# Attention stage A/B of a streaming encoder: the planner's TensorE order replaced by one written out by hand, with row-half scores

## The chip, the cores and the metric

The kernel runs on one core of a Trainium2 chip. The metric is the device time in microseconds (us) of one execution. TensorE does matmuls and transposes, VectorE (DVE) and ScalarE (ACT) do elementwise work, GpSimd (POOL) helps a little, SyncE (SP) issues most transfers.

## The reference

One inference step of a two-layer encoder for a prompt of 256 frames and a sample of 32 frames, which share all weights; the kernel treats them as one matrix of T = 288 columns, features on the partitions. Cut to what matters here, layer 0 is:

```python
qa, ka, va, qb, kb, vb, fl = split(rmsnorm(x) @ w_in)        # 8 heads A, 8 heads B, head_dim 64
qa, ka, qb, kb = per-head rmsnorm with gains
oa = softmax(qa @ ka.T / 8 + relative-position bias, band of chunks) @ va
ob = softmax(qb @ kb.T / 8 + c_q - c_k, causal) @ vb         # c: running sum of log f
x  = x + concat(oa, ob) @ w_out
x  = x + cross_attention(rmsnorm(x), memory keys and values) # 256 memory tokens, 4 heads of 256
x  = x + squared_relu_mlp(rmsnorm(x))
```

The sample also attends to 256 cached keys and values. Layer 1 has a stick-breaking attention of 16 heads (stage C) in place of A and B. New keys, values, log f and memory keys and values are outputs too.

## The kernel before, in words

**Products.** Each weight matrix is cut into chunks of 1024 x 256. `load_chunk` fetches a chunk in two halves (SP queue, four `raw` buffers), and ScalarE and VectorE split it into a high part `wh` and a low part `wl` (lines 143 and 144; three half-chunk tiles of each). `mm3` (lines 158 to 160) adds high x high, high x low and low x high, so one chunk is 2 column halves x 8 k x 3 = 48 matmuls of 288 columns ("slots" below). The results lie in `ps_g`, three banks, tile name `g`; a chunk uses two. VectorE evacuates them and applies `rs`, the row norm, which is worked out beside the first products.

**Stages.** ab (layer 0's attention), x0 (cross-attention), m0 (MLP), c, x1, m1. `phase` opens each stage's buffers. In ab the PSUM's eight banks are: three `ps_g`, one `ps_t`, two `R.s` (scores), one `R.m` (norms), one `R.o` (values).

**Stage A/B.** Four groups, A0, A1, B0, B1, of four heads (two pairs p of two heads par). `ORD_AB` lists the steps: q projects queries and keys (two chunks), p values, F the forget gate, a the attention of a group, M splits the memory, N its norm, K0 to K3 memory keys. The list is only the order in which instructions are written; the planner of the framework orders all engines' instructions itself, from modelled times, TensorE's too. `project_qk` makes per-head norms with `headnorm` (squares, split by `two_parts`, two matmuls against a block-diagonal of ones into `ps_hn`), and writes each query pair twice, once per head, with the other head's 64 rows zero (`qz`, line 438, gains `qg` that hold zeros). So `attend_ab` computes a head's scores with all 128 rows (lines 546 and 547), one bank for a head; `softmax_rows` adds the bias and takes maxima (L487), negates (L489), exponentiates (L491), takes reciprocals (L492) and normalises (L494, one instruction for each piece of a head). Three transposes of a head go to `ps_t` (L552 to L554), ScalarE copies them (`pt`), and `pv_prompt` (L503) multiplies by values into `po`, two heads in the two column halves. Sample scores (`ss`, L535, L536) and values (`pos`, L513) are done for a group at once.

**Stage C.** Here the order of TensorE alone is written out by hand, under `tc.manual_schedule`. A `Mix` object holds a generator of projections; `fill(n)` issues n slots of it, `until(key)` goes on until a result is there, and `later(n, fn)` runs a piece of work n slots on. `attend_c` keeps a pair's scores in two banks (`zz`), with unpadded queries: head e uses rows 64e to 64e+63 of both operands (line 692). Lines 695, 703, 737 and 738 are triangular sums that only this attention has.

## Time and profile before

| what | value |
|---|---|
| median of 3 runs | 965.09 us (964.53 to 966.41) |
| profiled execution | 964.98 us, span 963.3 us |
| stage A/B, first product to last of the output projection | 5.3 to 195.6 us |
| stage C, the same | 493.0 to 660.5 us |
| TensorE busy | 947.7 us, 98% |
| VectorE, ScalarE busy | 685.9 us (71%), 526.3 us (55%) |
| granted TensorE clock | 0.998 |

A row of a group reads: line, engine, operation, output <- inputs, shapes, count | busy us, mean ns | idle before, and what ended it. A timeline row reads: start us, duration us, engine, line, operation, count; rows of matmuls overlap, since a matmul starts before the one before it has ended, so the distance of two starts is what a matmul takes from TensorE. An fp32 matmul is recorded twice, once for each pass.

### The profile page before, as it was taken

To read this page: it belongs to the slowest core of one execution; us is meant where nothing else is said; L and a number is where in the kernel's file an instruction comes from. 1 tells how busy PE (TensorE), PEld (TensorE's weight loads), DVE (VectorE), ACT (ScalarE), POOL (GpSimd) and SP (SyncE) were. 2 spreads that over 40 slices of the span, in tenths; PEclk is the share of its full clock that TensorE was granted. 3 is DMA by queue.
4 is the path that set the end of the run, shared out by engine and by line. 5 is a ranking of instruction groups with operands and counts; after the bars stand their busy time and mean duration, and the time that the engine had idled before them with its cause. 6 is when DMAs were issued, how large, how long until landed. Compare 5 with 4: busy or idle time off the path is not lost.

```text
span 963.3 us, 19227 instructions
## 1 busy us (share of the span) xinstructions
PE 947.7 (98%) x7284; PEld 916.5 (95%) x7284; DVE 685.9 (71%) x1506; ACT 526.3 (55%) x1220; POOL 172.3 (18%) x200
## 2 busy tenths in 40 slices
PE   8999999999999999999999999999999999999998
PEld 7988889899999999999999999999999999999998
DVE  8779978769678766767687567778977756465643
ACT  5667767556456645444465647564554655454531
POOL 4002200021212221222100000003444212111110
PEclk9999999999999999999999999999999999999999
DMA  8654464644555454545564454465453555545452
GB/s 265 208 155 138 140 213 156 216 159 138 171 170 172 158 173 158 172 159 169 165 206 163 143 164 134 155 210 185 132 165 124 162 178 163 168 160 174 156 174 72
DMA packets 50701, 160.01 MB, mean 166 GB/s; under 512 B 6297, under 2 KB 12969, under 8 KB 50353
## 3 DMA queue, kind: packets, MB, share of 16 engines
q1 hardware_dynamic: 46864, 148.69, 48.1%
q0 software_dynamic: 2592, 8.92, 2.4%
q10 hardware_dynamic: 1152, 1.18, 0.4%
q8 instruction: 57, 0.93, 0.4%
q14 instruction: 36, 0.29, 0.1%
HBM read 148.65 MB, written 10.12 MB: 165 GB/s over the span
## 4 chain that ended last, share of the span: by engine, by line
PE 88%; DVE 6%; DMA 2%; ACT 2%; issue 1%; SPq 0%; DVEq 0%; ACTq 0%
PE g L158 26%; PE g L160 26%; PE g L159 26%; DVE wl L144 2%; DMA raw<-in_w_kv_dram 1%; PE po L503 1%; PE zz L737 1%; PE zz L692 1%; PE zz L503 1%; ACT wh L143 1%; DMA bsmp<-cd 0%; ACT pr L491 0%; DMA raw<-in_ab_w_dram 0%; DVE spl L725 0%; PE sx L158 0%
## 5 line engine op out<-in xcount | busy, mean ns | idle before, releaser
L143 ACT ACTIVATE wh<-raw 128x512 fp32r<-128x512 f32 (+3 forms) x541 | 269.1, 547 | 243.5 <-PE g L159 132.9
L144 DVE TENSOR_TENSOR wl<-raw,wh 128x512 fp32r<-128x512 f32 (+3 forms) x519 | 319.9, 653 | 98.9 <-ACT wh L143 92.6
L158 PE MATMUL g<-xh,wh 128*128 128x288 f32 (+1 forms) x1032 | 304.2, 299 | 4.5 <-DVE qz L626 1.9
L159 PE MATMUL g<-xl,wh 128*128 128x288 f32 (+1 forms) x1032 | 303.5, 296 | 2.2 <-DVE xl L196 2.2
L160 PE MATMUL g<-xh,wl 128*128 128x288 f32 (+1 forms) x1032 | 302.4, 297 | 0.4 <-DVE wl L144 0.4
L144 POOL TENSOR_TENSOR wl<-raw,wh 128x256 fp32r<-128x256 f32 (+2 forms) x105 | 123.3, 1174 | 438.2 <-ACT wh L143 348.1
L158 PEld LDWEIGHTS g<-xh,wh 128*128 128x128 f32 (+1 forms) x1032 | 192.1, 187 | 8.3 <-DVE vT L465 2.2
L159 PEld LDWEIGHTS g<-xl,wh 128*128 128x128 f32 (+1 forms) x1032 | 192.8, 188 | 3.6 <-DVE xl L196 3.1
L160 PEld LDWEIGHTS g<-xh,wl 128*128 128x128 f32 (+1 forms) x1032 | 192.5, 188 | 2.6 <-DVE wl L144 1.4
L159 PE MATMUL g<-hl,wh 128*128 128x288 f32 x512 | 150.3, 295 | 0.0
L158 PE MATMUL g<-hh,wh 128*128 128x288 f32 x512 | 148.9, 295 | 0.0
L160 PE MATMUL g<-hh,wl 128*128 128x288 f32 x512 | 148.5, 294 | 0.0
L159 PEld LDWEIGHTS g<-hl,wh 128*128 128x128 f32 x512 | 96.1, 188 | 0.0
L160 PEld LDWEIGHTS g<-hh,wl 128*128 128x128 f32 x512 | 95.7, 188 | 0.0
L158 PEld LDWEIGHTS g<-hh,wh 128*128 128x128 f32 x512 | 95.3, 187 | 0.0
L159 PE MATMUL g<-ol,wh 128*128 128x288 f32 x256 | 75.2, 296 | 0.0
L158 PE MATMUL g<-oh,wh 128*128 128x288 f32 x256 | 74.1, 296 | 0.3 <-ACT oh L522 0.3
L160 PE MATMUL g<-oh,wl 128*128 128x288 f32 x256 | 74.1, 295 | 0.0
L141 DVE CAST wh<-raw 128x256 fp32r<-128x256 f32 (+2 forms) x83 | 32.4, 391 | 40.7 <-PE g L159 21.3
L889 DVE TENSOR_TENSOR h<-h,g 128x288 f32<-128x288 f32 x64 | 28.8, 450 | 29.6 <-PE g L160 29.5
L159 PEld LDWEIGHTS g<-ol,wh 128*128 128x128 f32 x256 | 48.1, 188 | 0.8 <-issue 0.8
L158 PEld LDWEIGHTS g<-oh,wh 128*128 128x128 f32 x256 | 47.5, 188 | 0.6 <-ACT oh L522 0.4
(285 smaller groups left out, 1471.8 us busy)
## 6 DMA issues: line engine op xcount, KB each, us to landing
raw<-in_w_up_dram SPq DMA_DIRECT2D x64, 512.0 KB, 3.8
raw<-in_w_down_dram SPq DMA_DIRECT2D x64, 512.0 KB, 3.8
raw<-in_w_kv_dram SPq DMA_DIRECT2D x32, 512.0 KB, 4.0
raw<-in_sb_w_dram SPq DMA_DIRECT2D x24, 512.0 KB, 4.2
raw<-in_ab_w_dram SPq DMA_DIRECT2D x22, 512.0 KB, 4.8
raw<-in_w_q_dram SPq DMA_DIRECT2D x16, 512.0 KB, 4.0
raw<-in_w_o_dram SPq DMA_DIRECT2D x16, 512.0 KB, 4.1
raw<-in_ab_wo_dram SPq DMA_DIRECT2D x8, 512.0 KB, 3.7
```

The lines of the kernel that those rows point to most:

```text
L141: dve.tensor_copy(wh[:, r, :], src)
L143: act(wh[:, r, :], src, AF.Copy)
L144: e.tensor_tensor(wl[:, r, :], src, wh[:, r, :].bitcast(F32), ALU.subtract)
L158: mm(out, lh, rh, start=first, stop=False)
L159: mm(out, lh, rl, start=False, stop=False)
L160: return mm(out, ll, rh, start=False, stop=last)
L503: mm(po[64 * par:64 * par + 64, kk * P:NP_], vt[:, kk, cols], pts[par][kk], start=kk == 0, stop=kk == 1)
L692: mm(block(zz, e, kk), kT[r, p, kk * P:(kk + 1) * P], qz[r, p, kk * P:NP_].rearrange("p (b c) -> p b c", c=P), start=kk == 0, stop=False, ...
L737: mm(zz[:, e, 0:384], mtrir, x[:, e, :], stop=False, **k_)
L889: dve.tensor_tensor(h[:, kt, :], h[:, kt, :], ps[:, 0:T], ALU.add)
```

## The change

- A and B get stage C's manner: `Mix` is made general (`run_ab` and `run_c` are its two generators), and TensorE's order from A0's scores to the last memory key is written out under `tc.manual_schedule`. The first query chunk stays with the planner.
- Queries are unpadded: one `qz` of 288 columns for a pair, gain `qg` for both heads. Scores of a pair go to a tile `zz` of two banks, head e by rows 64e to 64e+63. The two transposed pieces and the values of the pair are written back into the same two banks.
- A pair's maxima, negations, sums and reciprocals share one [128, 4] tile, and its normalisation is two tensor_tensor instructions with the reciprocals broadcast.
- Projections come in pieces of 6 or 12 slots between attention steps (`FILL_AB`), and head norms follow their projection by 18 and 30 slots (`FILL_HN`). Keys of A0, and of C's group 0, are projected one column half after the other (`one_by_one`).
- Caches and biases of a group are fetched by `ready_ab` one group ahead; A0's before its keys' weights.
- `R.m` and `R.o` are gone from stage ab: norms use `ps_t`.
- The step list has keys and values apart, and all attention between them by the fills. Unused switches are removed.

```diff
-ORD_AB = 'qA0 pA0 F qA1 pA1 aA0 qB0 aA1 qB1 pB0 M pB1 aB0 N K2 aB1 K0 K3 K1'.split()
+ORD_AB = 'qA0 kA0 vA0 F qA1 kA1 vA1 qB0 kB0 vB0 M qB1 kB1 vB1 N K2 K0 K3 K1'.split()
+FILL_AB = 72, 30, 24, 12
+FILL_HN = 18, 30
...
-        if kind[0] != "c":
+        if kind[0] == "x":
             R.m = R.stack.enter_context(tc.tile_pool(name="m_" + kind, bufs=1, space=PS))
             R.o = R.stack.enter_context(tc.tile_pool(name="o_" + kind, bufs=1, space=PS))
...
+        def products(self, ap, xh, xl, n=T, ws=None, one_by_one=False):
...
+            if one_by_one:
+                for d in range(2):
+                    for k in range(0, KT, 4):
+                        part(d, k, k + 4)
+                        yield 12
+            else:
+                for k0, k1 in ((0, 1), (1, 2), (2, 4), (4, 6), (6, 8)):
+                    for d in range(2):
+                        part(d, k0, k1)
+                    yield 6 * (k1 - k0)
...
+        def qk(ap, tag, gain, then, **kw):
+            out = R.ph.tile([P, 2, T], F32, tag=tag, name=tag, bufs=QZB)
+            yield from mix.products(ap, xh, xl, **kw)
+            for p in range(2):
+                t = R.ph.tile([P, T], F32, tag="tn", bufs=4, name="t")
+                dve.tensor_tensor(t, mix.ps[p][:, 0:T], rs, ALU.mult)
+                sq = scr.tile([P, T], F32, tag="f", bufs=FB, name="sqh")
+                act(sq, t, AF.Square)
+                parts = two_parts(sq, T)
...
+                mix.later(FILL_HN[p], ...norm_head...)
...
+    def attend_ab(kind, g, qz, kT, vt, ck, cv, b1, b0, bsmp, oh, ol, fill):
...
+        for p in range(2):
+            zz = R.s.tile([P, 2, 512], F32, tag="zz", name="zz")
+            for lo, n, q0 in ((0, NP_, P), (NP_, P, 0)):
+                for e in range(2):
+                    r = slice(64 * e, 64 * e + 64)
+                    mm(zz[:, e, lo:lo + n], qz[r, p, q0:q0 + P], kT[r, p, 0:n], start=True, stop=True)
...
+        def norm_pair(pr, ri):
+            for j, (lo, n) in enumerate(((0, NP_), (NP_, P))):
+                x = pr[:, :, lo:lo + n]
+                dve.tensor_tensor(x, x, ri[:, 2 * j:2 * j + 2].unsqueeze(2).to_broadcast([P, 2, n]), ALU.mult)
...
+        fill(FILL_AB[0])
+        for p, (zz, pr) in enumerate(pairs):
+            for e in range(2):
+                for c, lo in enumerate((NP_, 0, P)):
+                    nc.tensor.transpose(zz[:, e, c * P:(c + 1) * P], pr[:, e, lo:lo + P], ident)
+            pt = R.ph.tile([P, 2, 384], F32, tag="pt", name="pt", bufs=2)
+            act(pt, zz[:, :, 0:384], AF.Copy)
+            if p == 0:
+                fill(FILL_AB[1])
...
+        fill(FILL_AB[2])
+        vt = vt()
+        for p, (zz, pr) in enumerate(pairs):
+            pv_prompt(zz[:, 0, :], p, vt, ...)
+            put_prompt(oh, ol, kt0 + p, zz[:, 0, :])
+        fill(FILL_AB[3])
...
+    mix = Mix(run_ab, ORD_AB, (xh, xl, rs))
+    mix.fill(48)
+    groups = [(0, 0), (0, 1), (1, 0), (1, 1)]
+    got = ready_ab(mix, *groups[0])
+    with tc.manual_schedule(engines={mybir.EngineType.PE}):
+        for n, (kind, g) in enumerate(groups):
+            at = "AB"[kind] + str(g)
+            qz, kT = mix.until(("q", at)), mix.until(("k", at))
+            mix.fill(18)
+            now, got = got, ready_ab(mix, *groups[n + 1]) if n < 3 else None
+            attend_ab(kind, g, qz, kT, lambda at=at: mix.until(("v", at)), *now, oh, ol, mix.fill)
+        mix.fill(1000)
```

## The prediction

> **What bounds the kernel now.** I read the page first: TensorE is busy all the time and carries the chain.

> ```profile
> span 963.3 us, 19227 instructions
> ...
> PE 947.7 (98%) x7284; PEld 916.5 (95%) x7284; DVE 685.9 (71%) x1506; ACT 526.3 (55%) x1220; POOL 172.3 (18%) x200
> ...
> GB/s 265 208 155 138 140 213 156 216 159 138 171 170 172 158 173 158 172 159 169 165 206 163 143 164 134 155 210 185 132 165 124 162 178 163 168 160 174 156 174 72
> ...
> PE 88%; DVE 6%; DMA 2%; ACT 2%; issue 1%; SPq 0%; DVEq 0%; ACTq 0%
> ```

> Busy says little about how densely TensorE works, so I counted products per stretch. The next view is busy time by stretch for the product tile g alone; (x...) is the number of matmuls. The rows are the A/B stage from the end of its first norm to the end of its output projection, the same of stage C, and 100 us of MLP.

> ```profile
> 18.75:195.69 176.94, 134.54 (x937) 123.61 (x936) 17.48 (x40) 1.00 0.55 181
> 492.96:660.64 167.68, 132.64 (x963) 126.21 (x962) 17.66 (x41) 1.00 0.52 169
> 340.00:440.00 100.00, 100.00 (x753) 100.00 (x753) 13.94 (x31) 1.00 0.52 165
> ```

> The MLP has nothing but 288-column products: 100/753 = 0.1328 us each, TensorE's floor for this kernel. In each attention stage four memory projections (192 products, from the code) have 256 columns; 24 of them in a row, first and last here, take 2.71/23 = 0.118 us each.

> ```profile
> 546.88 0.27 PE L158 MATMUL g<-mh,wh 128*128 128x256 f32 x1
> ...
> 549.59 0.28 PE L160 MATMUL g<-mh,wl 128*128 128x256 f32 x1
> ```

> So A/B's products need 745 x 0.1328 + 192 x 0.118 = 121.6 us, and 176.94 - 121.6 = **55.3 us** go to everything else: scores, transposes, values, norms, switches between kinds, waits. C's products need 771 x 0.1328 + 22.7 = 125.1 us, and only **42.6 us** are left, although C has triangular matmuls that A/B lacks. C already has the manual order that the change gives to A/B, so C is the measure.

> The waits of TensorE in those two stretches (C's opening last):

> ```profile
> PE g L158 <- DVE vT L465: 1.7, 1, 1.7
> PE ps_pt L552 <- ACT pt L556: 1.1, 2, 0.9
> PE pos L513 <- ACT pts L565: 0.9, 1, 0.9
> PE ps_hn L349 <- DVE sl L343: 0.6, 1, 0.6
> ...
> PE g L158 <- DVE qz L626: 1.9, 1, 1.9
> ```

> Plain waits in A/B are under 5 us; the rest of its 55.3 us is work that is issued dearly. Timeline rows of A/B (start, duration, record count):

> ```profile
> 139.61 0.65 PE L503 MATMUL po<-pt,vt 128*64 128x256 f32 x2
> 140.19 0.70 PE L546 MATMUL s<-kT,qz 128*128 128x256 f32 x2
> 140.72 0.38 PE L547 MATMUL s<-kT,qz 128*128 128x128 f32 x2
> 140.86 0.36 PE L158 MATMUL g<-mh,wh 128*128 128x256 f32 x1
> ...
> 143.06 0.86 PE L503 MATMUL po<-pt,vt 128*64 128x256 f32 x6
> 143.85 0.33 PE L552 MATMUL ps_pt<-ident,pr 128*128 128x128 f32 x1
> ...
> 144.24 0.60 PE L546 MATMUL s<-kT,qz 128*128 128x256 f32 x2
> ```

> One head's scores hold TensorE from 140.19 to 140.86, 0.67 us. The values of a pair are torn: one column half alone (139.61 to 140.19, 0.58) and the others later (143.06 to 143.85, 0.79), together 1.37. Three transposes with their switch take 0.39. The same kinds in C, and C's own triangular work:

> ```profile
> 511.64 0.92 PE L692 MATMUL zz<-qz,kT 64*128 64x256 f32 x8
> 512.50 0.50 PE L695 MATMUL zz<-mtrir,big 128*128 128x256 f32 x2
> 512.93 0.92 PE L692 MATMUL zz<-qz,kT 64*128 64x256 f32 x8
> ...
> 528.50 0.34 PE L737 MATMUL zz<-sph,mtrir 128*128 128x384 f32 x1
> ...
> 530.76 0.50 PE L744 MATMUL ps_ws<-ident,ws 128*128 128x128 f32 x3
> ...
> 535.17 1.52 PE L503 MATMUL zz<-w,vt 128*64 128x256 f32 x16
> 536.62 0.40 PE L158 MATMUL g<-xh,wh 128*128 128x288 f32 x1
> ```

> Two heads' row-half scores take 0.86 us (511.64 to 512.50), two pairs' unbroken values 1.45.

> **The change part by part.**

> *Order of A/B, whole.* Take C's remainder, remove what A/B will not have, add what C has not. C's own: the block 528.50 to 530.76, 2.26 x 4 groups, and 0.43 x 8 pairs for big, together 12.5; the opening wait 1.9. Left: 42.6 - 14.4 = 28.2 us for scores, sample scores, values, v transposes, memory norms, switches. A/B adds the 32 head-norm matmuls at 0.1328 = 4.25, 16 triples of transposes at 0.39 = 6.2, and about 1 us for the memory's row sums (an estimate: six matmuls). After: 28.2 + 11.5 = 39.7 instead of 55.3: **-15.6 us**. The pieces agree: scores 8 x (2 x 0.67 - 0.86) = 3.8; values up to 4 x (2 x 1.37 - 1.45) = 5.2; the waits above 4.3; the remaining 2 or 3 us are fewer switches between kinds.

> *VectorE and ScalarE.* VectorE is what could take this back. Busy time of all engines (PE, PEld, DVE, ACT, POOL) in A/B, C, and A/B's fullest 30 us, and groups of A/B:

> ```profile
> 18.75:195.69 176.94, 172.06 (x1325) 157.20 (x1324) 139.91 (x399) 117.48 (x312) 21.66 (x29) 1.00 0.55 181
> 492.96:660.64 167.68, 165.33 (x1349) 157.03 (x1348) 116.73 (x225) 97.59 (x196) 9.79 (x19) 1.00 0.52 169
> 85.00:115.00 30.00, 29.11 (x235) 24.44 (x234) 28.09 (x99) 21.61 (x63) 7.32 (x9) 1.00 0.38 124
> ```

> ```profile
> L144 DVE TENSOR_TENSOR wl<-raw,wh 128x512 fp32r<-128x512 f32 x75 | 49.5, 690 | 10.9 <-ACT wh L143 10.9
> L438 DVE SCALAR_TENSOR_TENSOR qz<-t,qg,r 128x288 f32<-128x288 f32 x16 | 7.5, 514 | 0.9 <-ACT r L183 0.8
> L487 DVE CUSTOM_DVE_ANT_0 pr<-s,b 128x256 f32<-128x256 f32 x16 | 6.7, 417 | 0.5 <-PE ps_pt L554 0.3 <-PE ps_pts L563 0.2
> L494 DVE TENSOR_SCALAR pr<-pr,ri 128x256 f32<-128x256 f32 x16 | 5.6, 349 | 0.1
> L494 DVE TENSOR_SCALAR pr<-pr,ri 128x128 f32<-128x128 f32 x16 | 4.6, 289 | 0.0
> L376 DVE TENSOR_TENSOR tmk<-g,memrs 128x256 f32<-128x256 f32 x8 | 3.2, 418 | 1.2 <-PE g L160 1.1
> L489 DVE TENSOR_SCALAR nm<-mx 128x2 f32<-128x2 f32 x16 | 2.6, 166 | 0.0
> ...
> L491 ACT ACTIVATE pr<-pr,nm 128x256 f32<-128x256 f32 x16 | 8.0, 502 | 6.9 <-DVE nm L489 6.9
> ```

> Unpadded queries drop 8 of 16 qz writes, 8 x 0.514 = 4.1 us. The normalisation goes from 16 x (0.349 + 0.289) = 10.2 to 8 x (0.690 + 0.418) = 8.9, priced by subtractions and products of the same 512 and 256 columns. Halving the maxima's negations and the reciprocals saves 8 x 2 x 0.166 = 2.7. VectorE's 139.9 falls to about 131.8, but over 176.9 - 15.6 = 161.3 us: 82%, where A/B now has 79% and C 70%.

> [...]

> What TensorE loses to a busier VectorE is not shown; the ends are 0 (it managed 28.09 of 30 us, 94%, in the fullest stretch; at 94%, 131.8 us need 140) and 6 us (A/B keeps its 79%: 131.8/0.79 = 167). I take **+3 us**, between C's near-absent waits and A/B's 4.3. The place is between B0's scores and the end: the memory split M stands there in program order ahead of B0's softmax, and the four memory projections follow.

> *Chains against fills.* A pair's softmax (four L487, negation, exponentials, normalisation) has 72 product slots, 9.6 us. On VectorE even both pairs and the sample need about 4 x 2 x 0.417 + 8.9/4 + 1.5 = 7 us; on ScalarE eight exponentials near 0.5 us run beside. Enough, cost zero; if VectorE is behind, this is in the 3 us.

> *Queues.* On SP, A0's caches and biases (1.17 MB by the tile sizes) now stand ahead of kA0's weights, before they were behind the first of them. At the first slice's 265 GB/s that is up to 4.4 us later; the first query projection still covers TensorE meanwhile, and what is delayed leaves later. I take 0, upper end 4. A1's and B's loads go out one group earlier than their use; the POOL work on B's biases moves with them, off the path. The manual order makes every wait hold all of TensorE; its one-bank tile ps_t now also serves head norms.

> *Stage C.* kC0 one column half at a time needs only the free bank for 24 slots, 3.2 us, which covers the 1.9 us wait on qz: **-1.9** (0 if its second weight half is late, next in line).

> Constants (qg, m01) cost nothing either way. Sum: -15.6 + 3 - 1.9 = -14.5 us. The profiled execution took 964.98 us (span 963.3), 0.1 under the median 965.09: **950.5 us**.

> [...]

> **The rivals.**
> 1. *VectorE becomes A/B's bound.* For it: 94% busy in 85:115 and 82% mean after. Against: it has three weight tiles of slack, and C's order never waits. Price: A/B ends with 6 to 10 us of waits instead of 3: 954 to 958. Chance 0.2.
> 2. *Slower: every group waits in line at ps_t.* Eight hand-overs per group pass one bank (four head norms, two v turns, sample scores, their transposes), about 38 in all; each needs its reader on ScalarE or VectorE, in order. From 0.46 us per hand-over (17.5/38) the gain is gone; at 0.6 us the time is 965 + 5 = 970. For it: VectorE's queue and the strict order. Against: C passes zs, v turns, sample and norms through the same bank with no listed wait. Chance 0.07.
> 3. *Nothing comes of it*: VectorE's 94% holds throughout and TensorE's dear pieces were idle time anyway: 965. Against: VectorE is 21% idle in A/B. Chance 0.05.
> 4. *VectorE costs nothing, and switches fall further*: 944. Chance 0.08.

> **How the numbers follow.** The forecast (947 to 954) has 0.6. The range leaves out most of rivals 2 and 3 and a little below: 943 to 959. About 0.2%, 1.9 us, is what a measurement here tells from no change. Faster: 0.6 + 0.2 + 0.08 and a little of case 3 = 0.89; within 0.2%: 0.04; slower: 0.07.

> **What would show it.** In the changed trace the A/B stage should end near 181 us (output projection's last product) instead of 195.7; scores should be zz matmuls of 64 rows, a pair in 0.86 us; values x16 unbroken; no wait on qz at C's start; VectorE near 82% in A/B. Wrong if TensorE's waits in A/B exceed 10 us, above all head norms or ps_t users waiting for ScalarE, or wl late after M.

## The result, and the profile after

The changed kernel takes 972.1 us (median of four runs, 971.6 to 972.9) against 965.8 for the kernel before beside it: a ratio of 1.0066, 95% interval 1.0051 to 1.0080. It is slower by 0.7%, where 950.5 us was forecast. The profiled execution took 971.62 us with a span of 969.9.

Two lines of the page, and the clock row, that answer to those of before:

```profile
span 969.9 us, 19190 instructions
PE 941.2 (97%) x7284; PEld 914.7 (94%) x7284; DVE 682.6 (70%) x1462; ACT 526.8 (54%) x1216; POOL 170.9 (18%) x200
PEclk9998999999999999999999999999999999999999
```

VectorE has 44 instructions fewer, as the change promises, and the clock row has an 8: in that slice (one fortieth of the span, 72.7 to 97.0 us) TensorE was granted less than full speed. The stretches show where. Busy time by stretch (columns: length, then busy time and count of PE, PEld, DVE, ACT and POOL, then the granted clock): A/B as a whole, then two windows in which TensorE mostly stood, each with the stretch behind it.

```profile
18.75:204.58 185.83, 166.12 (x1325) 156.04 (x1325) 137.62 (x360) 118.51 (x309) 20.38 (x28) 0.96 0.53 175
87.99:91.40 3.41, 0.97 (x8) 0.73 (x6) 3.39 (x4) 2.47 (x6) 2.68 (x2) 1.00 0.00 0
91.40:98.23 6.83, 5.00 (x19) 4.71 (x20) 4.15 (x10) 1.36 (x3) 0.00 (x0) 0.50 0.48 150
...
125.53:128.94 3.41, 0.88 (x6) 0.88 (x7) 2.86 (x9) 3.41 (x13) 0.00 (x0) 1.00 0.00 0
128.94:132.35 3.41, 3.41 (x17) 3.41 (x16) 2.90 (x7) 2.21 (x6) 0.00 (x0) 0.50 0.45 138
```

A/B ends at 204.58 instead of 195.69 us: 8.9 us later, all of the loss and more. After a window in which TensorE mostly stood (0.97 of 3.41 us busy) the next runs at half clock. Two neighbouring products of the last stretch:

```profile
129.22 0.44 PE L143 MATMUL g<-xh,wl 128*128 128x288 f32 x1
129.46 0.44 PE L141 MATMUL g<-xh,wh 128*128 128x288 f32 x1
```

They start 0.240 us apart, where at full clock 100.00 us hold 754 such products (340 to 440 us, clock 1.00), 0.133 each: 45% of the time in which TensorE works at half clock is lost. There are three such stretches (from 23.13, 91.40 and 128.94 us; 3.41, 6.83 and 3.41 us long). TensorE works in them for 3.41 + 5.00 + 3.41 = 11.8 us, so they cost some 5.3 us. Between 18.75 us and A/B's end the kernel before has none.

TensorE's waits in A/B (engine, tile and line, what released it: us in all, times, longest):

```profile
PE ps_hn L326 <- DVE sh L319: 4.0, 1, 4.0
PE ps_vt L379 <- DVE mx L635: 3.5, 2, 3.2
PE g L141 <- ACT wh L132: 2.7, 1, 2.7
PE ps_hn L326 <- ACT r L164: 2.6, 1, 2.6
PE ps_xn L327 <- DVE sl L321: 1.3, 1, 1.3
PE ps_cq L982 <- DVE c L976: 1.2, 1, 1.2
PE ps_ms L313 <- ACT memrs L164: 1.0, 1, 1.0
PE g L143 <- DVE wl L133: 1.0, 1, 1.0
...
```

With the five smaller rows they come to 20.2 us (0.6 of it ahead of 18.75), against 4.8 for all rows of before. The busy columns agree: TensorE is idle for 185.83 - 166.12 = 19.7 us, against 176.94 - 172.06 = 4.9 before. So A/B's account is 166.12 - 5.3 = 160.8 us of work, against 172.06 before. **The work did become some 11.2 us cheaper; 14.8 us of new idle time and some 5.3 us of half clock took it back.** The pieces themselves, two pairs' scores, a pair's transposes and a pair's values:

```profile
117.94 1.58 PE L618 MATMUL zz<-kT,qz 64*128 64x256 f32 x16
...
105.42 0.82 PE L661 MATMUL zz<-ident,pr 128*128 128x128 f32 x6
...
109.84 1.52 PE L417 MATMUL zz<-pt,vt 128*64 128x256 f32 x16
```

A pair's scores take 1.58/2 = 0.79 us, values run unbroken. Stage C went from 167.68 to 165.49 us.

The three large losses, in order of time. First, the start. SP's queue (start, length of the issue):

```profile
11.41 0.35 SPq L386 DMA_DIRECT2D ck<-in_cakT_dram  x1
11.80 0.65 SPq L388 DMA_DIRECT2D cv<-in_cav_dram  x1
12.50 0.59 SPq L580 DMA_DIRECT2D b<-in_biasp_dram  x1
13.13 0.43 SPq L583 DMA_DIRECT2D bsmp<-in_biass_dram  x1
13.61 1.98 SPq L115 DMA_DIRECT2D raw<-in_ab_w_dram  x3
```

A0's caches and biases stand ahead of kA0's weights (raw, 13.61), and TensorE waits at 18.1 us for the first split of them (`g <- ACT wh`, 2.7), then for its lower half (`wl`, 1.0); the half-rate stretch from 23.13 us follows.

Second, A1's softmax. Rows of the timeline, of ScalarE, VectorE, GpSimd and TensorE:

```profile
78.69 0.51 ACT L291 ACTIVATE mh<-mraw,gT 128x256 fp32r<-128x256 f32 x1 [1.93 <-DMA mraw<-in_memT_dram]
...
81.56 0.51 ACT L291 ACTIVATE mh<-mraw,gT 128x256 fp32r<-128x256 f32 x1 [0.86 <-DMA mraw<-in_memT_dram]
```

```profile
81.52 0.87 DVE L292 SCALAR_TENSOR_TENSOR ml<-mraw,gT,mh 128x256 fp32r<-128x256 f32 x2
82.31 0.45 DVE L635 CUSTOM_DVE_ANT_0 prs<-ss,bsmp 128x288 f32<-128x288 f32 x1
...
84.06 1.03 DVE L646 TENSOR_TENSOR pr<-pr,ri 128x512 f32<-128x512 f32 x2
...
88.01 3.01 DVE L646 TENSOR_TENSOR pr<-pr,ri 128x512 f32<-128x512 f32 x2
...
92.49 0.30 DVE L319 CAST sh<-sqh 128x288 fp32r<-128x288 f32 x1
```

```profile
87.22 2.06 POOL L594 TENSOR_TENSOR b<-b,cq 128x1024 f32<-128x1024 f32 x1
89.35 1.40 POOL L595 TENSOR_SCALAR_AFFINE_SELECT b<-b 128x1024 f32<-128x1024 f32 x1
```

```profile
82.82 0.44 PE L379 MATMUL ps_vt<-ident,vT 128*128 128x128 f32 x2 [3.24 <-DVE mx L635]
...
92.93 0.58 PE L326 MATMUL ps_hn<-sh,bdr 128*128 128x288 f32 x1 [3.97 <-DVE sh L319]
```

M's first step (L291) stands on ScalarE within A1's softmax and waits there for its own transfer, 1.93 and 0.86 us; its lower halves (ml) stand on VectorE ahead of the maximum of the sample scores (82.31). Until that has read the bank of ps_t, the transposes of v can't begin (wait of 3.24). VectorE is then so far behind that the head norm's sh is ready 3.97 us late. Part of that lag falls beside GpSimd, which adds forget sums to a B group's bias and masks it from 85.43 to 90.75 us: the second pair's normalisation (88.01) takes 3.01 us there, the first pair's (84.06) 1.03, and two of M's steps take 1.75 us where two at 81.52 take 0.87. Experiment 8 tries what GpSimd costs.

Third, B0. ScalarE's and TensorE's rows:

```profile
126.50 0.52 ACT L639 ACTIVATE prs<-prs,nm 128x288 f32<-128x288 f32 x1
127.02 0.61 ACT L132 ACTIVATE wh<-raw 128x512 fp32r<-128x512 f32 x1
127.53 0.48 ACT L164 ACTIVATE r<-ps_hn,epsb 128x288 f32<-128x288 f32 x1
```

```profile
123.59 0.30 PE L327 MATMUL ps_hn<-sl,bdr 128*128 128x288 f32 x1
128.06 0.40 PE L326 MATMUL ps_hn<-sh,bdr 128*128 128x288 f32 x1 [2.58 <-ACT r L164]
```

The first head norm's sum is there at 123.9, but its logarithm (L164) stands behind nine exponentials that ScalarE runs from 122.97 on; the second head norm needs the same bank and waits 2.58 us.

### The profile page after: what moved, and what is told of

Same layout as the page of the kernel before. It is cut to its first block, busy times and chain, and to the rows that moved or that the text cites. A ratio compares the mean times of both kernels' runs of the same rounds, so it can differ in the third digit from the quotient of the medians.

```text
span 969.9 us, 19190 instructions
## 1 busy us (share of the span) xinstructions
PE 941.2 (97%) x7284; PEld 914.7 (94%) x7284; DVE 682.6 (70%) x1462; ACT 526.8 (54%) x1216; POOL 170.9 (18%) x200
## 4 chain that ended last, share of the span: by engine, by line
PE 87%; DVE 6%; DMA 3%; ACT 2%; issue 1%; SPq 0%; DVEq 0%; ACTq 0%
PE g L141 26%; PE g L143 26%; PE g L142 26%; DVE wl L133 2%; PE zz L417 1%; ACT pr L639 1%; DMA raw<-in_ab_w_dram 1%; PE zz L783 1%; PE zz L738 1%; PE zz L427 1%; DMA h<-in_xT_dram 0%; DMA mraw<-in_memT_dram 0%; DVE spl L771 0%; PE sx L141 0%; PE sx L143 0%
## 5 line engine op out<-in xcount | busy, mean ns | idle before, releaser
L143 PE MATMUL g<-xh,wl 128*128 128x288 f32 (+1 forms) x1032 | 304.0, 298 | 3.0 <-DVE wl L133 3.0
L141 PEld LDWEIGHTS g<-xh,wh 128*128 128x128 f32 (+1 forms) x1032 | 194.1, 189 | 6.5 <-ACT wh L132 2.9
L143 PEld LDWEIGHTS g<-xh,wl 128*128 128x128 f32 (+1 forms) x1032 | 194.3, 189 | 5.0 <-DVE wl L133 4.2
L143 PE MATMUL g<-hh,wl 128*128 128x288 f32 x512 | 148.6, 294 | 0.0
L143 PEld LDWEIGHTS g<-hh,wl 128*128 128x128 f32 x512 | 95.7, 188 | 0.0
L143 PE MATMUL g<-oh,wl 128*128 128x288 f32 x256 | 73.6, 295 | 0.0
```

Of the source, the lines that this page charges most:

```text
L141: mm(out, lh, rh, start=first, stop=False)
L143: return mm(out, ll, rh, start=False, stop=last)
```

## The experiments

**1. kA0's weights first** (e1_keys_first).

```
-    got = ready_ab(mix, *groups[0])
...
+            qz = mix.until(("q", at))
+            if n == 0:
+                got = ready_ab(mix, *groups[0])
```

> The changed kernel, but A0's caches and biases are issued after qA0's products instead of before them, so that kA0's two weight transfers stand ahead of them in SP's queue. Theory 1 (the gain of the dear pieces is lost to waits behind in-order queues and to the half-rate clock that follows each of them): TensorE's two waits at 17.85 and 21.06 us (2.84 and 1.17 us) and the half-rate stretch at 23.13 (3.41 us, some 1.7 lost) go, except what the sample scores then wait for the caches; 3 to 5.5 us off, 966.5 to 969. Rival (VectorE's throughput sets the end of A/B): the wait only moves to a later product, at most 1 us off, 971 to 972.5.

Measured: 968.4 us, 3.7 under the changed kernel; against before 1.0032 (1.0018 to 1.0046). No wait for wh, wl above 0.4 us is left at the start, and no half-rate stretch there. As theory 1 says. Its half-rate time in A/B is 13.65 us all the same, at other places: what went is wait.

**2. M spread and held** (e5_m_spread; `held` queues each step behind the last traced ScalarE and VectorE instruction).

```
-                mix.mem = mem_split(0)
+                mix.mem = mem_split(0, lambda k, fn: mix.later(12 * k + 6, lambda: held(fn)))
```

> The changed kernel, but the memory split M isn't free to run ahead: its eight steps are written 12 TensorE slots apart and each is queued on ScalarE and VectorE behind what was written before it, so that none stands in A1's softmax. Theory 1 (waits in in-order queues plus half rate): the waits at 79.29, 85.07 and 88.67 us (3.4, 0.7 and 4.1) and the half-rate stretch at 91.4 (6.83 us, 3.4 lost) go; up to 11.6 us off, less up to 4 for what M delays behind B0: 960.5 to 965. Rival (VectorE's throughput is the bound): the same work of VectorE takes the same time elsewhere, within 1.5 us of the changed kernel, 970.5 to 973.

Measured: 974.3 us (969.9 to 975.1), not better than the changed kernel. A miss for theory 1 as it was put. The waits at the transposes of v did go (3.5 to 0.6), but TensorE stands in the same stretch all the same, at the next thing that VectorE makes: 1.7 us for sh at 85.0 and 3.1 for sl at 87.0.

**3. Both** (e7_keys_m).

> Both edits at once: kA0's weights ahead of A0's caches in SP's queue, and M's steps spread and held. Theory 1: the two savings add, 955.5 to 962, and the end of A/B comes at 188 to 194 us instead of 204.5, with no half-rate stretch before 120 us but that of the start. Rival (VectorE's throughput): the sum is less than half of the two single savings, or 969 to 973.

Measured: 968.5 us; 1.0023 (1.0004 to 1.0043). A miss again: M's part adds nothing to e1. What VectorE does there instead, in its rows and in GpSimd's:

```profile
81.72 1.15 DVE L319 CAST sh<-sqh 128x288 fp32r<-128x288 f32 x1
82.78 0.68 DVE L133 TENSOR_TENSOR wl<-raw,wh 128x512 fp32r<-128x512 f32 x1
83.39 0.88 DVE L321 TENSOR_TENSOR sl<-sqh,sh 128x288 fp32r<-128x288 f32 x1
84.19 2.38 DVE L133 TENSOR_TENSOR wl<-raw,wh 128x512 fp32r<-128x512 f32 x1
```

```profile
81.20 1.50 POOL L600 TENSOR_TENSOR b<-b,cq 128x512 f32<-128x512 f32 x1 [12.30 <-DMA b<-cd]
82.77 1.19 POOL L601 TENSOR_SCALAR_AFFINE_SELECT b<-b 128x512 f32<-128x512 f32 x1
83.93 2.09 POOL L600 TENSOR_TENSOR b<-b,cq 128x1024 f32<-128x1024 f32 x1
```

sh takes 1.15 us and ends at 82.87, 0.17 after GpSimd's sum has ended; wl takes 2.38 and ends at 86.57, 0.55 after the second sum: neither ends before the sum beside it. So two causes were open: the softmax's nine rows at once with head norms that come too soon behind them, and GpSimd.

**4. Stage C alone** (b1_c_only: the kernel before, with k0's products one output half at a time).

> The kernel before with only one part of the change, in stage C: k0's products one output half after the other, in four pieces of twelve. If that alone made the 2.2 us that C gained (theory): 963.0 to 964.2 against 965.5 for the kernel before. Rival (C gained by its other start, since the weights that A/B leaves behind or the buffers for q changed with it): within 0.5 us of the kernel before.

Measured: 962.6 us; 0.9979 (0.9968 to 0.9990). Stage C takes 656.88 - 491.35 = 165.53 us instead of 167.68, the same as with the whole change, and TensorE's wait for qz at its start is gone. The time lies 0.4 us below the theory's range.

**5. Head norms farther** (e8_keys_hn with M as in the change, e6_three with M spread; both with kA0's weights first).

```
-FILL_HN = 18, 30
+FILL_HN = 36, 48
```

> kA0's weights first (as in e1_keys_first) and each head norm's sums written 36 and 48 TensorE slots behind the products they belong to, instead of 18 and 30; M as in the changed kernel. Theory 1, now put as a matter of distance (a hand-written distance in TensorE slots is shorter than the queue on VectorE and ScalarE at that place, so TensorE stands, and the clock halves after): the 6.3 us of waits at the head norms' bank that e1_keys_first still has, and two of its half-rate stretches (1.7 us each), go; the 4.1 at the transposes of v, with the 6.83 us half-rate stretch behind them, stay: 959 to 964, against 968.4 of e1_keys_first. Rival (VectorE's throughput): the waits come back at the next score group, whose keys come later; 967 to 969.5.

> kA0's weights first, M's steps spread and held, and the head norms' sums 36 and 48 slots behind. Theory 1 by distances: e7_keys_m still waits 8.1 us at the head norms' bank and has two half-rate stretches behind them (3.4 us); they go, and 957 to 962 is left, against 968.5. Rival (throughput, or the keys that are now late): 966 to 969.5.

Measured: 964.1 us (960.4 to 965.2), 0.9980 (0.9963 to 0.9996), and 958.2 (956.6 to 962.2), 0.9931 (0.9903 to 0.9960). e6 is within what the distances gave, e8 just above its upper edge. Here M's spread is worth 964.1 - 958.2 = 5.9 us (3.6 between executions of like clock, 0.996 or more: 960.5 and 956.9 in the middle), where with the short distances it was worth nothing (968.4 and 968.5). So one cause covered the other: M's mend shows only once the distances are mended, though these alone show 4.3 us.

**6. Two more distances** (e9_all).

```
-        mix.later(66, turn)
+        mix.later(90, turn)
-FILL_AB = 72, 30, 24, 12
+FILL_AB = 72, 30, 24, 24
```

> As e6_three, and the turn of the forget sums 90 slots behind instead of 66, and 24 instead of 12 slots between a group's prompt values and its sample values. Theory 1 by distances: the two single waits at ps_cq (1.2 us) and at the sample values (1.6) go as well: 954.5 to 960. Rival: the later turn delays B's bias and the sample values the output projection; no better than e6_three.

Measured: 956.0 us; 0.9895 (0.9868 to 0.9922). A/B ends at 188.94.

**7. The order left to the scheduler** (e3_planner: all of the change but `manual_schedule` in A/B).

> All of the change, but A/B's TensorE instructions are left to the scheduler, as in the kernel before, instead of standing in the order in which they are written. If the hand-written order is what loses the gain (theory 1: its distances don't fit what VectorE and ScalarE do there): A/B ends near 185 to 192 and the time is 952 to 962. Rival (the pieces themselves, a pair's nine softmax rows coming at once, cost it in any order): 967 to 975.

Measured: 967.0 us; 1.0008 (0.9994 to 1.0023), A/B ending at 198.13. The time lies on the edge of the rival's range: the scheduler's order gains 5 us on the hand-written one with its first distances, but e9_all's order by hand, with the other mends, is 11 us faster still. So it isn't the hand-written order as such that cost the gain. The scheduler's order with the same mends wasn't run.

**8. Without GpSimd's bias work** (p1_no_pool).

> e7_keys_m (968.5 us) without the four GpSimd instructions that work each B group's forget sums and causal mask into its bias tiles; that part of the computation is left out. Theory (GpSimd's elementwise work holds VectorE's up while both run): beside it e7_keys_m shows sh in 1.15 us, sl in 0.88 and one wl in 2.38, where 0.36, 0.46 and 0.68 are usual in the same stage; without it these go back to the usual lengths, the two waits at the head norms' bank at 81.4 and 83.0 us (2.5 us together) and the half-rate stretch behind them (1.7) go: 964 to 966.5. Rival (VectorE's instructions are long there for their operands, or its queue alone is late): the lengths stay, and the time is within 1 us of 968.5.

Measured: 962.6 us, 5.9 under e7_keys_m, more than expected; 0.9972 (0.9962 to 0.9982) against before. The same instructions now:

```profile
80.12 0.30 DVE L319 CAST sh<-sqh 128x288 fp32r<-128x288 f32 x1
80.76 0.69 DVE L133 TENSOR_TENSOR wl<-raw,wh 128x512 fp32r<-128x512 f32 x1 [0.33 <-ACT wh L132]
81.37 0.45 DVE L321 TENSOR_TENSOR sl<-sqh,sh 128x288 fp32r<-128x288 f32 x1
81.73 0.69 DVE L133 TENSOR_TENSOR wl<-raw,wh 128x512 fp32r<-128x512 f32 x1
```

0.30, 0.45 and 0.69 us, with the same operands: the lengths are as the theory says. Of the two waits, 2.2 us in the trace of e7_keys_m, only 0.9 went; a wait of 1.6 us at 67.05 us, beside GpSimd's work on the other group, and the half-rate stretch at 84.3 us are gone too. These make up most of the 4.5 us between the two profiled executions; the rest of the 5.9 isn't accounted for. The kernel before has this work at 80.6 to 86.5 and 101.5 to 106.5 us, beside VectorE as well, and its TensorE waits in A/B come to 4.8 us all the same.

**9. M later still, and distances farther still** (e10_m_later: M written behind qB1; e11_far: that, and `FILL_HN = 42, 60`).

> As e9_all (956.0 us), with M's spread steps begun behind qB1's products instead of vB0's, so that they fall behind B0's softmax rather than into it. Theory 1 by queues: the two waits at 109.8 and 113.0 us (1.2 and 2.2) shrink and the half-rate stretch at 115.56 (1.7) goes: 951.5 to 954.5. Rival (B0's nine exponentials alone hold the head norm's logarithm back, M or not): 955 to 957.

> As e10_m_later, with the head norms' sums 42 and 60 slots behind their products instead of 36 and 48, so that the second of a pair comes 18 slots (2.4 us) behind the first and doesn't wait in line for the one bank. Theory 1 by distances: the waits at the head norms' bank still left after e10_m_later (some 2 to 4 us) go, 949.5 to 953. Rival (the keys, and with them the next scores, now come too late): e10_m_later or up to 2 us slower.

Measured: 959.4 us (0.9940; 0.9923 to 0.9956) and 967.3 (1.0018; 1.0001 to 1.0034). Both miss: 3.4 and 11.3 us slower than e9_all. One row of the waits of each:

```profile
PE ps_ms L310 <- DVE mssum L299: 2.9, 1, 2.9
```

```profile
PE ps_ms L310 <- DVE mssum L299: 5.6, 1, 5.6
```

M now ends too late for N, the sum of the memory's squares, which the order by hand places at a fixed slot. At half rate e10 spends 6.83 us in A/B, e11 13.65.

**10. N moved, and q's distance alone** (e12_n_late is e10 and e13_n_late9 is e9, with N 30 slots into K2's products; e15_q_far is e13 with 48 and 66 for q alone).

```
-                mem_rms(mix.mem[2])
-                yield 4
+                mix.later(30, lambda: mem_rms(mix.mem[2]))
...
-                mix.later(FILL_HN[p], ...norm_head...)
+                mix.later((FILL_HN if tag == "kT" else (48, 66))[p], ...norm_head...)
```

> As e10_m_later (959.4 us), but N (the sum of the memory's squares over partitions) is written 30 slots into K2's products instead of ahead of them. If e10 lost its 3.4 us to e9_all by that sum coming too late for N's place (2.9 us of wait at 123.5 us and a half-rate stretch of 6.83 us behind it, 3.4 lost): 952.5 to 955. Rival (M in kB1's and vB1's stretch costs that much anywhere): 957.5 to 960.

> As e9_all (956.0 us), with N written 30 slots into K2's products. By the two waits at N that e9_all shows (0.74 and 0.86 us over): 954 to 955.3. Rival (they are only handed on to the next wait): 955.5 to 956.5.

> As e13_n_late9, with the head norm's sums of q 48 and 66 slots behind their products; those of k stay at 36 and 48. Theory (crowding at the one bank: the second of a pair waits until ScalarE has read the first): the waits at 80.6, 109.8 and 113.0 us (1.7, 1.2 and 2.2) shrink by at least half, and the half-rate stretch goes: 950 to 953. Rival (q's and k's norms now meet in the same stretch, and crowd there): 954 to 957. The 11 us that e11_far lost would then be put down to the keys, which here come no later.

Measured: 956.5 us (0.9903; 0.9878 to 0.9927), 955.8 (0.9899; 0.9879 to 0.9920) and **953.0** (952.6 to 954.4; 0.9876, 0.9856 to 0.9895). e12 gets back 2.9 us of the 3.4 that e10 lost, and lies between the two ranges: most of that loss was N's place, and two waits of 0.6 us are left at ps_ms. e13 is within the rival's range: nothing that can be told from e9. e15 gains 2.8 us with q's norms farther out, at the upper end of the theory's range. The half-rate stretch that e13 has from 132.24 us is gone (e15's A/B runs at full clock; ahead of the kernel's end it has one stretch, in the opening, from 12.35). The waits shrank less than the theory said, from 9.1 to 7.2 us in all, and those for r at the head norms' bank from 4.1 to 3.3: crowding at the bank is only part of them. That most of what e11 lost beyond N lay with its later keys fits, since q alone farther out gains, but no run tried it by itself. e15's A/B stage and waits:

```profile
18.75:185.97 167.22, 160.06 (x1323) 150.31 (x1323) 134.31 (x358) 116.89 (x307) 22.53 (x29) 1.00 0.58 191
```

```profile
PE ps_hn L326 <- ACT r L164: 3.3, 3, 1.3
PE ps_pts L674 <- ACT r L164: 1.1, 1, 1.1
PE ps_hn L326 <- ACT cq L988: 1.0, 1, 1.0
...
```

The waits are down to 7.2 us in all, and A/B ends at 185.97 us. This version beats both kernels: 1.2% under the one before.

## Why the prediction was wrong

*The order of A/B, -15.6.* The mechanism and the size were right: 4.3 of it were waits, and the other 11.3 compare with 11.2 by the account above, and with 172.06 - 160.06 = 12.0 in e15, whose A/B ran at full clock. Scores as 64-row zz matmuls, values x16, no wait at C's start: all as foretold. The end near 181 us was not: 204.58, and 185.97 in the best version. (By the terms for A/B alone, -15.6 + 3, it would have been 183; 181 takes in stage C's 1.9 us.)

*VectorE, +3 with ends 0 and 6.* This is the term that failed, together with "Chains against fills ... cost zero". Three us of waits were allowed; the rows show 20.2, and these 17 us with the half clock's 5.3 make up the 21.6 us between forecast and result within 1 us. The prediction compared VectorE's busy time with the stretch (82%), and 4 x 2 softmax instructions with 9.6 us of fill, as if the queue held nothing else. It holds, in those 9.6 us, also the weights' lower halves, t, sh and sl, M's steps, and what GpSimd's sums add beside them (the normalisation at 88.01 took 3.01 us, the one at 84.06 1.03). In the best version the same work of VectorE makes 134.31/167.22 = 80% of the stage, about the 82% foretold, and TensorE waits for VectorE for 0.3 us in all: rival 1 (throughput) is refuted. What counts is whether one result is there at the slot where TensorE, whose order is fixed, comes to it.

*The place.* The prediction looked for M "ahead of B0's softmax", where it is written. TensorE alone follows the written order; on ScalarE and VectorE the scheduler put M's steps from 78.69 us on, into A1's softmax.

*Queues, 0 with upper end 4.* A0's caches ahead of kA0's weights cost 3.7 us by experiment 1: the upper end was the value. "The first query projection still covers TensorE" didn't hold.

*GpSimd, "moves with them, off the path".* VectorE's instructions took longer beside its work: in e7_keys_m one wl 2.38 us and sh 1.15, which take 0.69 and 0.30 without that work (p1_no_pool), and taking it out was worth 5.9 us; in the changed kernel a normalisation took 3.01 us beside it (at 88.01). In the changed kernel alone it wasn't taken out, so its share there is open.

*The granted clock* had no term. The profile of before shows one half-rate stretch, at 7.52 us, behind 3.41 us of the opening in which TensorE stood for 1.91; the prediction didn't ask what the clock does behind a wait. In the changed kernel three such stretches added some 5.3 us to 20.2 of waits. The expectations that put 1.7 us on a stretch of 3.41 priced it a little high: 45% of it is 1.5.

*Stage C, -1.9.* Right: -2.2, and -2.15 by that edit alone.

*Rival 2* (970 us, chance 0.07) is where the time came out, and it is partly what happened: rows at ps_t's bank (ps_hn, ps_vt, ps_xn, ps_cq, ps_ms) make 15 of the 20.2 us. But not as 38 like hand-overs of 0.5 us: three of them make 9.8, and half of the 15 (7.6) wait for an operand that VectorE makes late, not for the bank. The prediction's own sign, waits over 10 us at head norms and the users of ps_t, is what showed.

By medians the mending goes 972.1, 968.4 (queue), 964.1 (head norms' distance), 958.2 (M), 956.0 (turn, sample values), 953.0 (N, q's distance): the gain forecast was there to be had, less some 2.5 us; the waits of 7.2 us that are left, where 3 were allowed, exceed that.

## What to carry to other kernels

When one engine's order is fixed by hand, price each hand-over by the queue of the engine that makes the operand at that place (everything in it, also what the scheduler may pull in there), not by that engine's mean load. A hand-written distance is a number to be measured: 18 slots more took e7_keys_m from 968.5 to 958.2 us, and 6 and 12 beyond that took e10 from 959.4 to 967.3. And where one cause covers another, mending the covered one alone shows nothing; mend both before a theory is dropped.

## What the runs showed of the hardware

*VectorE's instructions beside GpSimd's sums.* In e7_keys_m sh takes 1.15 us and one wl 2.38, ending 0.17 and 0.55 us after GpSimd's sum; in p1_no_pool, without that work, the cast takes 0.30 and the subtraction 0.69. It isn't every instruction beside GpSimd: the wl at 82.78 keeps its 0.68, and GpSimd's mask, which starts with it, takes 1.19 us where e6_three shows 0.64 (at 61.34 us). By what path GpSimd's work lengthens them, no run shows.
